# Moving operands that begin 12 bytes into their tiles, and another order of the three passes

## The chip, the core and the metric

The kernel runs on one core of one Trainium2 chip. The metric is the time of one execution on the device, in microseconds (us); a time is the median of several runs. Of the core's engines, TensorE multiplies (its rows read PE, and PEld for loading weights), VectorE (DVE), ScalarE (ACT) and GpSimd (POOL) work element by element, and SyncE (SP) and POOL issue most of the transfers (DMA) between the chip's memory and the on-chip memory, which has 128 partitions.

## What is computed

One step of a decoder layer in float32, for 512 tokens of a new sequence and 8 single tokens of running ones, 520 columns in all: a norm; a projection of 2048 channels to 6160 columns; a short gated convolution on one part and gated linear attention with 4 heads on the other; an output projection with residual; a norm; a gated feed-forward part with a causal convolution and 5632 channels; its down projection with residual; a last norm.

```python
def trunk(x, ...):
    m, c_new, s_new = mixer(rmsnorm(x, norm_mix_g[l]), ...)      # proj = xn @ w_in; out = concat(ya, yb) @ w_out
    x = x + m
    f, f_new = conv_ffn(rmsnorm(x, norm_ffn_g[l]), ...)          # u, v = split(xn @ w_up); h = silu(conv(u) + b) * v; h @ w_down
    x = x + f
    return rmsnorm(x, final_norm_g), ...
```

Nearly all the work is in four products: activations with `w_in`, `w_out`, `w_up` and `w_down`.

## The kernel before

**Three passes per product.** Every float32 number that goes into a large product is split in two parts of the type float32r: hi is the number rounded to it (ScalarE), lo what is left (VectorE). A product of weights w and activations x is then the sum of three matmuls, wh·xh + wh·xl + wl·xh, added up in one bank of the accumulator. In a matmul the weights, 128 x 128, are loaded into the array first (one LDWEIGHTS for each MATMUL in the program), and the activations move through it, 260 columns at a time: half of the 520. The activations are the *moving operand*. They lie in tiles of 128 partitions and T = 520 columns; the second half starts 260 columns, 1040 bytes, into the tile. As the program lays out its memory, each of these tiles starts at a multiple of 32 bytes in its partition, and so each half at a multiple of 16.

**Three places issue these passes.** `mm3` (L140) serves the first part of the kernel, the plain input projection, with two halves for each pass, and the last part, a remainder of the down projection in parts of 264 and 256 columns. `up_product` (L1218) serves the rest of the input projection ("mix") and the up projection, `chunk_product` (L1461) the output and the down projection. The latter two use a scheme with seven products instead of eight for a 2 x 2 block of matrices (Strassen's, in the form with few sums): a group of weights gives seven products, numbered in `ORDER`, each of 24 matmuls: eight steps of 128 rows, three passes each (`up_product`), or four steps with two column blocks (`chunk_product`).

**Which tiles move.** `pair_tiles` makes a pair of tiles, hi and lo, for the normed input (`bh`, `bl`, `ch`, `cl`, `xh`, `xl`). `form` gives the sums of activation blocks that the seven products need (`bh`, `yh`, `yl`, `b` in the profile's names); `load_form` loads such sums from memory, in the output and down projections, into tiles called `form`. The tiles of `form` and `load_form` share their places with others: those of `mixer_sums` ("yx") and the running sums `acc` of the projections. `tmp` is the pool of short-lived tiles. `keep_last` saves the last rows of the convolutions' inputs: it gathers them in a tile `last`, transposes it, copies it to `flat` on ScalarE and stores it.

**Order.** Behind the first part the order of each engine's work is written out: `prepare(i + 2)` makes the hi and lo parts of the weights two products ahead of their use, each product's `finish` empties the banks, and `run_steps` deals out the smaller work between products. A class `InOrder` fixes that order on TensorE, VectorE and ScalarE, later on POOL and SP too; in the first part a scheduler may still exchange steps.

Of the kernel before, what the change touches and what calls it, by code (L numbers as in the profile page):

```python
# [9 lines left out]
F32 = mybir.dt.float32  # L10
F32R = mybir.dt.float32r
# [6 lines left out]
P = 128  # L18
# [4 lines left out]
T = NP + NS  # L23
# [14 lines left out]
def trunk_kernel(  # L38
# [13 lines left out]
    tp = ctx.enter_context(tc.tile_pool(name="tmp", bufs=8))  # L52
# [37 lines left out]
                self.last[i.engine] = i.name  # L90

    def tmp():
        return tp.tile([P, T + 2], F32, tag="t", name="t")

    def two(ap):
        return ap.rearrange("p (a b) -> p a b", a=2)
# [34 lines left out]
    def halves(t):  # L131
        return t[:, :HT], t[:, HT:T]

    def mm3(outs, lhs, acts, first, last):

        wh, wl = lhs
        xh, xl = acts
        for i, (w, x) in enumerate(((wh, xh), (wh, xl), (wl, xh))):
            for o, xx in zip(outs, x):
                nc.tensor.matmul(o, w, xx, start=first and i == 0, stop=last and i == 2)  # L140

# [54 lines left out]
    bigA = actx.enter_context(tc.tile_pool(name="bigA", bufs=1, side="right"))  # L196
    bctx = ctx.enter_context(ExitStack())
    b12p = bctx.enter_context(tc.tile_pool(name="b12", bufs=1))

    def pair_tiles(pool, tag):  # L200

        return [pool.tile([P, T], F32R, tag=f"{tag[0]}{s}{tag[1:]}", name=tag[0] + s) for s in "hl"]

    xa, xw = [], {}
    for k in range(KD):
# [71 lines left out]
    with ExitStack() as es:  # L277
# [173 lines left out]
        for k in range(KD):  # L451
            c, t = k // 4, k % 4
# [117 lines left out]
    zp = actx.enter_context(tc.tile_pool(name="zpads", bufs=1, side="right"))  # L570
    yt1 = actx.enter_context(tc.tile_pool(name="yt1", bufs=1, side="right"))
# [4 lines left out]
    last = [None]  # L576
# [5 lines left out]
    def keep_last(z, j, n, new_p, new_s, get=None):  # L582

        jj = j % n
        if jj == 0:
            last[0] = zp.tile([P, 10, n], F32, tag=f"last{n}", name="last", bufs=2)
        if get:
            nc.scalar.activation(last[0][:, :, jj], z[:, NP:], AF.Copy)
        else:
            nc.gpsimd.tensor_copy(last[0][:, :, jj], z[:, NP:])  # L590
        if jj == n - 1:
            lt, c0 = last[0], (j - n + 1) * P

            def out():
                ps = (get or bank)()
                nc.tensor.transpose(
                    ps[: 10 * n, :P], lt.rearrange("p r j -> p (r j)"), idn
                )
                flat = zp.tile([110, P], F32, tag="flat", name="flat", bufs=2)
                nc.scalar.activation(flat[: 10 * n, :], ps[: 10 * n, :P], AF.Copy)  # L600
                for r in range(10):
                    dst = new_p[0, 0, r] if r < 2 else new_s[0, r - 2, 1]
                    (nc.gpsimd if get else nc.sync).dma_start(
                        dst[c0 : c0 + n * P].rearrange("(j p) -> j p", p=P),
                        flat[r * n : (r + 1) * n, :],
                    )

            soon.append(lambda: None)
            soon.append(out)
# [17 lines left out]
    slots = [None] * KD  # L627
    forms_d, xd = {"wo": g_d}, {}

    def load_form(kind, c, j):  # L630

        home = (7 * c + j) % 8
        if kind == "down" and home in (0, 7):
            home = 7 - home
        parts_ = []
        for x in range(2):
            tiles = []
            for q in range(2):
                t = slots[2 * home + q].tile(
                    [P, T], F32R, tag=f"y{'hl'[x]}{2 * home + q}", name="form"  # L640
                )
                pool = x == 1 if c == 0 else kind == "wo"
                (nc.gpsimd if pool else nc.sync).dma_start(
                    two(t.bitcast(F32)),
                    forms_d[kind][c][PLACE[ORDER[j]], x, 2 * q : 2 * q + 2].rearrange(
                        "i p c -> p i c"
                    ),
                )
                tiles += halves(t)
            parts_.append(tiles)  # L650
        xd[kind, c, ORDER[j]] = list(zip(*parts_))
# [11 lines left out]
    def acc_tag(n):  # L663
        return f"x{'hl'[n % 2]}{8 + n // 2}"
# [5 lines left out]
    def form(f, g):  # L670

        if f == 1:
            x = pair_tiles(bigA, f"b{g}")
        elif f in (2, 3):
            x = [
                bigA.tile([P, T], F32R, tag=acc_tag(4 * g + q), name="b2")
                for q in ((0, 3) if f == 2 else (1, 2))
            ]
        else:
            k = homes.get((f, g), {5: 0, 4: 4, 6: 8, 7: 12}[f] + g)  # L680
            x = [slots[k].tile([P, T], F32R, tag=f"y{s}{k}", name=f"y{s}{k}") for s in "hl"]
        for j, q in enumerate(zip(*(halves(y) for y in x))):
            xq[f, 2 * g + j] = q
        return x

    def first_tile(kind, g, m):

        return 4 * g + 2 * m if kind == "down" else 2 * g + 8 * m
# [6 lines left out]
    def mixer_sums():  # L695

        def place(n):
            return yt1.tile([P, T], F32, tag=f"y{n}", name="yx")  # L700

        for g in (1, 2, 3, 0):
            xg = [place(n) for n in ("l0 h8 l8 h0" if g % 2 else "l1 l4 h4 h0").split()]
            for q, x in enumerate(xg):
                nc.sync.dma_start(two(x), rows_of(xT_d, "mix", g, q))
            yield
            for q, x in enumerate(xg):
                m = first_tile("mix", g, q // 2)
                for j, h in enumerate(halves(x)):
                    nc.scalar.activation(h, h, AF.Copy, scale=gmix[:, m + j : m + j + 1])  # L710
                if q == 1:
                    yield
            yield
            t1, t3, t4, b22 = xg
            t2 = place("h1")
            sub(t1, t1, t3)
            minus(t2, t1, b22)
            yield
            if g:
                for f, t in ((5, t1), (4, t2)):  # L720
                    nc.gpsimd.dma_start(mt_d[f - 4, g], t)
            sub(t3, b22, t3)
            minus(t4, t2, t4)
            yield
            nc.gpsimd.dma_start(mt_d[3, g], t4)
            if g:
                nc.gpsimd.dma_start(mt_d[2, g], t3)
        for f, t in ((5, t1), (6, t3), (4, t2)):
            split(t, *form(f, 0))
# [32 lines left out]
    with ExitStack() as mix:  # L762
# [44 lines left out]
        with ExitStack() as gl:  # L807
# [263 lines left out]
            for h in range(NH):  # L1071
# [3 lines left out]
                k = gp.tile([P, T], F32, tag="qk", name="k", bufs=5)  # L1075
# [3 lines left out]
                q = gp.tile([P, T], F32, tag="qk", name="q", bufs=5)  # L1079
# [6 lines left out]
                for d in range(2):  # L1086
                    ps = group(w_in, 4096 + h * DV + d * P, xa, None if h + d else v0)
                    t = gp.tile([P, T], F32, tag="v", name="v", bufs=2)
# [119 lines left out]
    def up_product(i):  # L1208
        kind, at, r = order[i]
        st = state[kind, at]  # L1210
        b = BANK[r]
        if b not in st["bank"]:
            st["bank"][b] = mm_bank()[:, :HT]
        wh, wl = (x.rearrange("p (k c) -> p k c", k=8) for x in (his.pop(i), los.pop(i)))
        for k in range(8):
            xh, xl = xq[INPUT[r], k]
            for j, (w, x) in enumerate(((wh, xh), (wh, xl), (wl, xh))):
                nc.tensor.matmul(  # L1218
                    st["bank"][b], w[:, k, :], x, start=b not in st["used"] and k == 0 and j == 0,
                    stop=k == 7 and j == 2, skip_group_check=True,  # L1220
                )
        st["used"].add(b)
# [196 lines left out]

    def new_sums(g):  # L1420
        for q in range(4):
            acc[g, q] = bigA.tile([P, T], F32, tag=acc_tag(4 * g + q), name="acc")

    def load_residual(g):

# [21 lines left out]
    acc, dnp = {}, [None, None]  # L1447

    def chunk_product(i):
        kind, (c, g), r = order[i]  # L1450
        st = state[kind, (c, g)]
        b = BANK[r]
        if b not in st["bank"]:
            st["bank"][b] = two_banks("xy"[(g + (b == "c")) % 2])
        ps = inner(st["bank"][b])
        wh, wl = (x.rearrange("p (k c) -> p k c", k=4) for x in (his.pop(i), los.pop(i)))
        for k in range(4):
            xh, xl = xd[kind, c, r][k]
            for m in range(2):
                for j, (w, x) in enumerate(((wh, xh), (wh, xl), (wl, xh))):  # L1460
                    nc.tensor.matmul(  # L1461
                        ps[:, m, :], w[:, k, m * P : (m + 1) * P], x,
                        start=b not in st["used"] and k == 0 and j == 0,
                        stop=k == 3 and j == 2, skip_group_check=True,
                    )
        st["used"].add(b)
# [201 lines left out]
    for i, (kind, at, r) in enumerate(order):  # L1668
        j, n = i % 7, i // 7
# [41 lines left out]
        if i in (0, 2, NW, NW + 2):  # L1711

            x = xq[1, 0][0]
# [11 lines left out]
        if kind == "wo":  # L1725
            c, g = at
# [20 lines left out]
        if kind == "down":  # L1747
            c, g = at
# [157 lines left out]
```

## Time and profile before

| | us |
|---|---|
| median of 3 runs | 2180.16 |
| lowest, highest | 2179.63, 2182.27 |
| span of the profiled execution | 2180.4 |
| TensorE busy in it | 2152.9 (99%) |
| VectorE, ScalarE, POOL busy | 1735.7, 1114.0, 438.1 |

The profiled execution is the span between its first and its last instruction; nothing else is in its time. In the profile a line such as `L1218 PE MATMUL mm<-yl,hi 128*128 128x260 f32 x1696` says: at line 1218 TensorE multiplies the moving tile `yl` with the weights `hi` into the bank `mm`, 1696 times. Matmuls overlap each other in the pipeline: the 0.28 us that a row gives for one is longer than the distance between two starts, so it is the distance that counts, read from start times or from the number of matmuls in a window.

### The profile page before, as it was taken

The page shows a single profiled execution, that of the slowest core. Times are in us where ns is not written, and L with a number is a line of the kernel's source. Part 1 is how long each engine was busy: PE and PEld are TensorE (multiplying, and loading weights), DVE is VectorE, ACT ScalarE, POOL GpSimd, SP SyncE. Part 2 cuts the span into 40 slices and gives each one's busy share as a digit, 9 for nine tenths or more (in the row PEclk, how much of TensorE's full clock was granted, in tenths as well). Part 3 has the DMA queues.
Part 4 walks back from the last instruction along what each step waited for, and adds up shares of the span by engine and source line. Part 5 has one row for each costly group of instructions (what it writes and reads, how often), then busy time and mean ns, then how long its engine had stood idle before and what let it go on. Part 6 is the DMA issues. An engine that isn't in the chain of part 4 may idle for free.

```text
span 2180.4 us, 43803 instructions
## 1 busy us (share of the span) xinstructions
PE 2152.9 (99%) x17751; PEld 2131.3 (98%) x17751; DVE 1735.7 (80%) x2298; ACT 1114.0 (51%) x1625; POOL 438.1 (20%) x625
## 2 busy tenths in 40 slices
PE   9999999999999999999999999999999999999997
PEld 8999999999999999999999999999999999999997
DVE  6346465578888897988888988998998778888886
ACT  6335435355544586555555555555555553444445
POOL 4213131121243321121221131122111310010000
PEclk9999999999999999999999999999999999999999
DMA  8545464387788996667676676676677886894734
GB/s 247 147 125 158 122 191 124 92 246 210 204 257 248 297 266 176 179 178 187 164 189 174 165 195 176 163 194 177 171 186 190 285 202 197 248 271 132 226 107 156
DMA packets 467163, 415.51 MB, mean 191 GB/s; under 512 B 21641, under 2 KB 426393, under 8 KB 466817
## 3 DMA queue, kind: packets, MB, share of 16 engines
q1 hardware_dynamic: 424081, 289.71, 46.5%
q0 software_dynamic: 42832, 122.93, 21.4%
q8 instruction: 139, 2.28, 0.4%
q14 instruction: 63, 0.52, 0.1%
q10 hardware_dynamic: 48, 0.07, 0.0%
HBM read 299.45 MB, written 80.31 MB: 174 GB/s over the span
## 4 chain that ended last, share of the span: by engine, by line
PE 88%; DMA 4%; DVE 3%; issue 1%; ACT 1%; POOL 1%; SPq 0%; ACTq 0%; DVEq 0%; POOLq 0%
PE mm L1218 34%; PE mm L140 16%; PE ms L1218 14%; PE y L1461 7%; PE x L1461 7%; PE f L1461 3%; PE e L1461 3%; PE ms L957 1%; DMA raw<-in_w_out_dram 1%; DMA form<-g_d 1%; DVE lo L1198 1%; DMA g_d<-fh 1%; DMA x_d<-acc 1%; DMA yl<-t_d 0%; DMA raw<-in_w_down_dram 0%
## 5 line engine op out<-in xcount | busy, mean ns | idle before, releaser
L1218 PE MATMUL mm<-yl,hi 128*128 128x260 f32 x1696 | 479.8, 283 | 3.6 <-DVE yl L124 3.6
L1218 PE MATMUL mm<-yh,hi 128*128 128x260 f32 x1696 | 480.5, 283 | 2.1 <-ACT ms L1228 1.8
L1218 PE MATMUL mm<-yh,lo 128*128 128x260 f32 x1696 | 479.8, 283 | 0.8 <-DVE lo L1198 0.8
L1194 ACT ACTIVATE hi<-raw 128x1024 fp32r<-128x1024 f32 x324 | 342.6, 1057 | 233.9 <-PE mm L1218 69.0
L1198 DVE TENSOR_TENSOR lo<-raw,hi 128x1024 fp32r<-128x1024 f32 x324 | 395.2, 1220 | 41.2 <-ACT hi L1194 40.7
L1198 DVE TENSOR_TENSOR lo<-s,hi 128x1024 fp32r<-128x1024 f32 x243 | 298.3, 1228 | 127.2 <-ACT hi L1194 121.9
L1194 ACT ACTIVATE hi<-s 128x1024 fp32r<-128x1024 f32 x243 | 256.9, 1057 | 217.2 <-DVE s L1139 80.2
L1218 PEld LDWEIGHTS mm<-yl,hi 128*128 128x128 f32 x1696 | 320.1, 189 | 4.2 <-DVE yl L124 4.2
L1218 PEld LDWEIGHTS mm<-yh,hi 128*128 128x128 f32 x1696 | 319.7, 189 | 2.7 <-ACT ms L1228 2.0
L1218 PEld LDWEIGHTS mm<-yh,lo 128*128 128x128 f32 x1696 | 320.4, 189 | 1.2 <-DVE lo L1198 1.2
L1218 PE MATMUL ms<-b,hi 128*128 128x260 f32 x1408 | 257.8, 283 | 0.0
L1218 PEld LDWEIGHTS ms<-b,hi 128*128 128x128 f32 x1408 | 218.5, 190 | 0.0
L1461 PE MATMUL x<-form,hi 128*128 128x260 f32 x1120 | 204.6, 283 | 0.8 <-DVE acc L1480 0.8
L1461 PE MATMUL y<-form,hi 128*128 128x260 f32 x1120 | 204.5, 282 | 0.5 <-DVE acc L1480 0.5
L1139 DVE TENSOR_TENSOR s<-s,raw 128x1024 f32<-128x1024 f32 x162 | 197.8, 1221 | 2.8
L1218 PE MATMUL ms<-b,lo 128*128 128x260 f32 x704 | 199.5, 283 | 0.0
L1461 PEld LDWEIGHTS x<-form,hi 128*128 128x128 f32 x1120 | 172.4, 188 | 1.2 <-issue 1.0
L1461 PEld LDWEIGHTS y<-form,hi 128*128 128x128 f32 x1120 | 172.5, 188 | 0.8 <-issue 0.7
L1461 PE MATMUL y<-form,lo 128*128 128x260 f32 x560 | 158.2, 283 | 0.8 <-DVE lo L1198 0.8
L1461 PE MATMUL x<-form,lo 128*128 128x260 f32 x560 | 158.1, 282 | 0.0
L112 DVE TENSOR_TENSOR lo<-raw,hi 128x1024 fp32r<-128x1024 f32 x76 | 93.7, 1238 | 78.2 <-ACT hi L111 71.6
L1218 PEld LDWEIGHTS ms<-b,lo 128*128 128x128 f32 x704 | 133.4, 190 | 0.0
(366 smaller groups left out, 5077.8 us busy)
## 6 DMA issues: line engine op xcount, KB each, us to landing
raw<-in_w_up_dram SPq DMA_DIRECT2D x176, 512.0 KB, 4.7
raw<-in_w_down_dram SPq DMA_DIRECT2D x96, 512.0 KB, 5.5
raw<-in_w_in_dram SPq DMA_DIRECT2D x92, 512.0 KB, 4.4
form<-f_d SPq DMA_DIRECT2D x126, 260.0 KB, 6.8
raw<-raw POOLq DMA_DIRECT2D x56, 512.0 KB, 5.5
f_d<-t POOLq DMA_DIRECT2D x80, 260.0 KB, 5.5
raw<-in_w_out_dram SPq DMA_DIRECT2D x32, 512.0 KB, 12.7
form<-g_d POOLq DMA_DIRECT2D x42, 260.0 KB, 7.7
```

The source lines that it names most:

```text
L112: nc.vector.tensor_tensor(lo, raw, hi.bitcast(F32), op=ALU.subtract)
L140: nc.tensor.matmul(o, w, xx, start=first and i == 0, stop=last and i == 2)
L957: nc.tensor.matmul(pb[:, c * 64 : (c + 1) * 64], L[:, c, :], rhs[:, c], start=True, stop=True,)
L1139: return lambda: nc.vector.tensor_tensor(out, x, y, op=ALU.add)
L1194: nc.scalar.activation(his[i], src, AF.Copy)
L1198: nc.vector.tensor_tensor(los[i], src, his[i].bitcast(F32), op=ALU.subtract)
L1218: nc.tensor.matmul(st["bank"][b], w[:, k, :], x, start=b not in st["used"] and k == 0 and j == 0, stop=k == 7 and j == 2, skip_group_check ...
L1461: nc.tensor.matmul(ps[:, m, :], w[:, k, m * P : (m + 1) * P], x, start=b not in st["used"] and k == 0 and j == 0, stop=k == 3 and j == 2, ...
```

## The change

Two things. First, each tile that is a moving operand is made three columns wider, T + 3, and used from its fourth column: the operand begins 12 bytes into the tile. A helper, `moving`, does this for the pairs, the forms and the loaded forms; tiles that share a place with one of these are made wider too but used from their start. Three tiles are made smaller so that all fit: `tmp` loses two unused columns, `last` has one size for both convolutions, and `flat` has one buffer instead of two. Second, in all three places the passes run as wh·xh, wl·xh, wh·xl.

```diff
     def tmp():
-        return tp.tile([P, T + 2], F32, tag="t", name="t")
+        return tp.tile([P, T], F32, tag="t", name="t")
...
-        for i, (w, x) in enumerate(((wh, xh), (wh, xl), (wl, xh))):
+        for i, (w, x) in enumerate(((wh, xh), (wl, xh), (wh, xl))):
...
+    def moving(pool, tag, name):
+        return pool.tile([P, T + 3], F32R, tag=tag, name=name)[:, 3:]
...
-        return [pool.tile([P, T], F32R, tag=f"{tag[0]}{s}{tag[1:]}", name=tag[0] + s) for s in "hl"]
+        return [
+            moving(pool, f"{tag[0]}{s}{tag[1:]}", tag[0] + s) for s in "hl"
+        ]
...
-            last[0] = zp.tile([P, 10, n], F32, tag=f"last{n}", name="last", bufs=2)
+            last[0] = zp.tile([P, 110], F32, tag="last", name="last", bufs=2)[:, : 10 * n]
+            last[0] = last[0].rearrange("p (r j) -> p r j", j=n)
...
-                flat = zp.tile([110, P], F32, tag="flat", name="flat", bufs=2)
+                flat = zp.tile([110, P], F32, tag="flat", name="flat", bufs=1)
...
-                t = slots[2 * home + q].tile(
-                    [P, T], F32R, tag=f"y{'hl'[x]}{2 * home + q}", name="form"
-                )
+                t = moving(slots[2 * home + q], f"y{'hl'[x]}{2 * home + q}", "form")
...
-                bigA.tile([P, T], F32R, tag=acc_tag(4 * g + q), name="b2")
+                moving(bigA, acc_tag(4 * g + q), "b2")
...
-            x = [slots[k].tile([P, T], F32R, tag=f"y{s}{k}", name=f"y{s}{k}") for s in "hl"]
+            x = [moving(slots[k], f"y{s}{k}", f"y{s}{k}") for s in "hl"]
...
-            acc[g, q] = bigA.tile([P, T], F32, tag=acc_tag(4 * g + q), name="acc")
+            acc[g, q] = bigA.tile([P, T + 3], F32, tag=acc_tag(4 * g + q), name="acc")[:, :T]
```

The same exchange of passes stands in `up_product` and `chunk_product`. On TensorE, in the first product of `up_product` (the tiles `bh` and `bl` move, `hi` and `lo` are the weights), the program before has:

```order
L1218 MATMUL mm<-bh,hi 128x260
L1218 MATMUL mm<-bl,hi 128x260
L1218 MATMUL mm<-bh,lo 128x260
L1218 MATMUL mm<-bh,hi 128x260
L1218 MATMUL mm<-bl,hi 128x260
L1218 MATMUL mm<-bh,lo 128x260
```

and the changed one, whose lines stand five further down:

```order
L1223 MATMUL mm<-bh,hi 128x260
L1223 MATMUL mm<-bh,lo 128x260
L1223 MATMUL mm<-bl,hi 128x260
L1223 MATMUL mm<-bh,hi 128x260
L1223 MATMUL mm<-bh,lo 128x260
L1223 MATMUL mm<-bl,hi 128x260
```

The pass with `lo` has moved from the third place to the second, the pass with `bl` from the second to the third. In `mm3`, on TensorE near the start of the program, each pass runs over two tiles (`bh` and `ch`), so each moves by two places. Before:

```order
L140 MATMUL mm<-bh,hi 128x260
L140 MATMUL mm<-ch,hi 128x260
L140 MATMUL mm<-bl,hi 128x260
L140 MATMUL mm<-cl,hi 128x260
L140 MATMUL mm<-bh,lo 128x260
L140 MATMUL mm<-ch,lo 128x260
```

and now:

```order
L140 MATMUL mm<-bh,hi 128x260
L140 MATMUL mm<-ch,hi 128x260
L140 MATMUL mm<-bh,lo 128x260
L140 MATMUL mm<-ch,lo 128x260
L140 MATMUL mm<-bl,hi 128x260
L140 MATMUL mm<-cl,hi 128x260
```

The number of matmuls and of weight loads is the same.

More of the change, by code (lines that the diff above doesn't have):

```diff
@@ L699, in place @@
         def place(n):
-            return yt1.tile([P, T], F32, tag=f"y{n}", name="yx")
+            return yt1.tile([P, T + 3], F32, tag=f"y{n}", name="yx")[:, :T]
         for g in (1, 2, 3, 0):
@@ L1216, in up_product @@
             xh, xl = xq[INPUT[r], k]
-            for j, (w, x) in enumerate(((wh, xh), (wh, xl), (wl, xh))):
+            for j, (w, x) in enumerate(((wh, xh), (wl, xh), (wh, xl))):
                 nc.tensor.matmul(
@@ L1459, in chunk_product @@
             for m in range(2):
-                for j, (w, x) in enumerate(((wh, xh), (wh, xl), (wl, xh))):
+                for j, (w, x) in enumerate(((wh, xh), (wl, xh), (wh, xl))):
                     nc.tensor.matmul(
```

## The prediction

> **What bounds the kernel now.** I read the clock and the busy shares first, then the stretch of the span with the least other trouble in it, then the chain that ended last, then what TensorE waits for, and in the end single matmuls.
>
> ```profile
> core 0: 2180.4 us, clock 0.995
> ```
> ```profile
> PE 2152.9 (99%) x17751; PEld 2131.3 (98%) x17751; DVE 1735.7 (80%) x2298; ACT 1114.0 (51%) x1625; POOL 438.1 (20%) x625
> ```
> ```profile
> 1000.00:1400.00 400.00, 400.00 (x3342) 400.00 (x3342) 355.71 (x478) 217.69 (x322) 82.42 (x120) 1.00 0.68 178
> ```
>
> TensorE is busy for 99% of the span at a granted clock of 0.995, so the throttle is out of the question. In the window of the up projection (columns: window, length, then busy time and count of PE, PEld, DVE, ACT and POOL, then granted clock, DMA share, GB/s) it is busy for all of 400.00 us, with 3342 matmuls: one starts every 400.00 / 3342 = 119.7 ns. VectorE is next with 355.71 us, 89%.
>
> The chain that ended last says the same without the overlap of busy times: runs of 96 matmuls in 11.51 us, 119.9 ns each.
>
> ```profile
> 1000.22 11.51 PE mm L1218 x96
> 1020.35 11.51 PE mm L1218 x96
> ```
>
> How many matmuls are of the kind that the change touches? The three lines that run the products, over the whole span (columns: window, length, PE busy and count, PEld busy and count, clock, DMA share, GB/s), L1218, L1461 and L140 in this order:
>
> ```profile
> 0.00:2181.00 2181.00, 1074.78 (x8904) 1072.06 (x8904) 0.99 0.68 191
> ...
> 0.00:2181.00 2181.00, 566.05 (x4704) 564.53 (x4704) 0.99 0.68 191
> ...
> 0.00:2181.00 2181.00, 426.22 (x3264) 402.12 (x3264) 0.99 0.68 191
> ```
>
> That is 8904 + 4704 + 3264 = 16,872 matmuls. At 119.7 ns they make 2020 us of the 2180.4. So the change is priced in one unit: **1 ns on the spacing of these matmuls is 16.9 us, 0.77% of the time.** Waits can hardly matter. TensorE's longest, in total, are:
>
> ```profile
> PE mm L1218 <- DVE yl L124: 3.6, 3, 1.9
> PE mm L1218 <- ACT ms L1228: 1.8, 1, 1.8
> ...
> PE mm L140 <- DVE bl L127: 1.1, 2, 0.9
> ...
> PE mm L1218 <- DVE lo L1198: 0.8, 2, 0.5
> ...
> PE y L1461 <- DVE lo L1198: 0.8, 1, 0.8
> ...
> PE mm L140 <- DVE lo L112: 0.5, 1, 0.5
> ```
>
> **What sets the spacing.** If it were a fixed cost per instruction it would be the same for every operand. It is not. These are five starts in each of two products of the same kind (and the next start in the first), 377 us apart:
>
> ```profile
> 478.83 0.28 PE L1218 MATMUL mm<-yl,hi 128*128 128x260 f32 x1
> 478.95 0.30 PE L1218 MATMUL mm<-yh,lo 128*128 128x260 f32 x1
> 479.09 0.28 PE L1218 MATMUL mm<-yh,hi 128*128 128x260 f32 x1
> 479.21 0.28 PE L1218 MATMUL mm<-yl,hi 128*128 128x260 f32 x1
> 479.32 0.28 PE L1218 MATMUL mm<-yh,lo 128*128 128x260 f32 x1
> 479.44 0.28 PE L1218 MATMUL ms<-xh,hi 128*128 128x260 f32 x1
> ...
> 855.75 0.28 PE L1218 MATMUL mm<-yl,hi 128*128 128x260 f32 x1
> 855.87 0.30 PE L1218 MATMUL mm<-yh,lo 128*128 128x260 f32 x1
> 856.01 0.28 PE L1218 MATMUL mm<-yh,hi 128*128 128x260 f32 x1
> 856.13 0.28 PE L1218 MATMUL mm<-yl,hi 128*128 128x260 f32 x1
> 856.24 0.28 PE L1218 MATMUL mm<-yh,lo 128*128 128x260 f32 x1
> ```
>
> Starts follow each other by 0.12, 0.14, 0.12 and 0.11 us in the first product, and by the same four numbers in the second. The shape is the same in all of them; only the operands' places differ. So where the operands lie costs something: 0.14 us here, and from 479.21 to 479.44 two in a row take 0.23 us, 115 ns each. Each matmul reads 260 columns while the next weights (PEld) are read beside it. I take it that the two reads get into each other's way, and that the average of 119.7 ns holds some such delay. This is inferred: the page names no such wait.
>
> Width has a price too. Here are the first and the last of 12 consecutive matmuls of 264 columns, then of 12 of 256, in the last stage:
>
> ```profile
> 2112.75 0.28 PE L140 MATMUL mm<-bl,hi 128*128 128x264 f32 x1
> ...
> 2114.09 0.28 PE L140 MATMUL mm<-bh,hi 128*128 128x264 f32 x1
> ```
> ```profile
> 2142.33 0.28 PE L140 MATMUL mm<-bl,hi 128*128 128x256 f32 x1
> ...
> 2143.62 0.28 PE L140 MATMUL mm<-bh,hi 128*128 128x256 f32 x1
> ```
>
> 1.34 / 11 = 121.8 ns against 1.29 / 11 = 117.3 ns: 4.5 ns for eight columns. Counted in steps of four columns (16 bytes) it is 2.25 ns for one more step, or, in proportion (119.7 / 65), 1.84 ns.
>
> **The change, part by part.**
>
> *The 12 bytes.* Before, every moving operand starts at a multiple of 16 bytes in its partition (a half is 260 x 4 = 1040 bytes, so its second half does too); after, all start 12 bytes past one. No matmul, weight load or byte is added. No row of the profile has such an operand, so its cost is bounded from both sides. Upper end: the read now lies over 66 steps of 16 bytes in place of 65. If each step costs as above, that is +1.84 to +2.25 ns, 31 to 38 us slower. Lower end: the reads of columns and of the next weights no longer step together, and all matmuls go at the 115 ns of the undisturbed pair: -4.7 ns, 79 us faster (VectorE's 355.71 us would then be 93% of the shortened window, so it would not bind). The two ends lie on either side of zero. The row that I lean on is the repeated one, which shows that place alone moves a spacing by 20 to 30 ns out of 120; a shift that all operands have in common against the weights is a change of just that kind. I take the middle of the two ends, (-4.7 + 1.84) / 2 = -1.4 ns: 16,872 x -1.4 = **-24 us**.
>
> *The order of the passes.* A step of three ran wh·xh, wh·xl, wl·xh and now runs wh·xh, wl·xh, wh·xl. The count is the same, and each pass has its own weight load before and after (17751 of both). What moves is when a part is first needed: wl one pass earlier (two in L140, whose passes run over two halves), xl as much later. The four waits for lo in the rows above grow by 0.12 us each, the one of L140 by 0.24: +0.6 us. The five waits for yl and bl shrink by 3 x 0.12 + 2 x 0.24: -0.8 us. Elsewhere lo is made two products ahead (2 x 24 x 0.12 = 5.8 us), which covers it. Net **0**. As a tile xl is now the last one read, so its reload may start one pass, 0.12 us, later; hidden behind the same 5.8 us. If the order also changes how reads meet, that is inside the 12-byte term, since the bounds there are on the spacing as a whole.
>
> *The loads into shifted tiles.* The form tiles are loaded to places 12 bytes further on.
>
> ```profile
> form<-f_d SPq DMA_DIRECT2D x126, 260.0 KB, 6.8
> form<-g_d POOLq DMA_DIRECT2D x42, 260.0 KB, 7.7
> ...
>   DMA form<-g_d: 2.4, 5
> ```
>
> The last row is what TensorE's forms waited for: 2.4 us in 5 waits, all in the output projection. Their bytes stay the same: I take **0**. If an unaligned landing took twice as long, each of the five waits would grow by up to 7.7 us, 38 us; the 126 loads of the down projection are issued a whole chunk ahead and stay hidden.
>
> *The room made for it* (narrower tmp tiles, one tag for "last", one buffer for "flat"): the one new wait is ScalarE's copy to "flat" on the stores of the group before. In the up projection groups of 11 tiles are 11 x 20.13 us (the two chain rows) = 221 us apart, so the stores have long landed. **0.**
>
> Sum: 2180.4 - 24 + 0 + 0 + 0 = 2156 us. The profiled execution's 2180.4 and the median of 2180.16 agree within 0.3 us, so nothing is carried over.
>
> A rule speaks against this. The Trainium skill, in "SBUF — State Buffer", Specifications (TRN2), says that SBUF is read in lines of 16 bytes, that at least two hits on a line are needed for full bandwidth, and that each crossing to a new line costs. By it the shifted operand touches one line more, and the first line gives a single element; the time would be that of the first rival below. The width rows agree with a price per four columns; no run before this one has a shifted start.
>
> **Rivals.**
>
> *One more step per matmul (slower).* The place is every matmul of L1218, L1461 and L140. The read is the limit, each 16-byte step costs 1.84 ns, and 66 replace 65: 16,872 x 1.84 = +31 us, 2211 us. For it: 117.3, 119.7 and 121.8 ns for 256, 260 and 264 columns are near one ratio (0.458 to 0.461 ns a column), as if nothing but steps counted. Against it: a spacing of 110 to 140 ns at one width is no fixed price per step. It decides if the extra step is paid in full and the delays stay as they are.
>
> *Only reshuffled (no change).* The delays depend on many places at once; a common shift swaps long ones for short ones, and the mean over hundreds of places stays at 119.7: 2180 us, give or take 4. For it: in the chain the runs of 96 matmuls take the same 11.51 us, so the mean is steady. Against it: a common shift against the weights is not a random one.
>
> The Trainium skill has a rule for this case as well: "TensorE: Matmul & The Clock Gate", Step-by-step, says that weights have a read port of their own and take no bandwidth from the running matmul. By it the shift would change nothing. [...]
>
> *The loads become the wait (slower).* The 38 us above on an unchanged spacing: 2218 us, from the point where a form lands later than its product. Against it: loads of whole rows, and only five waits.
>
> **How the numbers follow.** Forecast 0.55, one more step 0.22, reshuffled 0.19, loads 0.04. The predicted time is the forecast's, 2156 us; its own range goes from 2101 (the lower end) to 2175. The range for all reaches up through no change to the slower cases, 2105 to 2205, and leaves out about 0.2. A difference of 0.2%, 4.4 us, is what a measurement of this kernel can tell. Faster: 0.55 and 0.03 of the reshuffled case, 0.58. Within 0.2%: 0.16, all but a little from reshuffling. Slower: 0.22, 0.02 and 0.02, 0.26.
>
> **What would show it.** In the window of the up projection the same 400 us should hold about 400 / 0.1183 = 3381 matmuls instead of 3342; the rival with one more step gives 400 / 0.1215 = 3292. Runs of 96 in the chain should take 11.38 us (rival: 11.69). Waits for lo and yl should differ by tenths of a microsecond, and waits for form should still be under 5 us. If the count per window stays at 3342 and the time moves all the same, the spacing was not the step and my reading is wrong.

## The result, and the profile after

The changed kernel takes 2171.28 us, the median of 5 runs (2168.1 to 2172.69), against 2181.0 us (5 runs, 2179.63 to 2182.27) for the kernel before on the same chip: a ratio of 0.9955, with the interval 0.9943 to 0.9966. It is faster by 9.7 us. The forecast was 24 us, two and a half times as much.

The span and clock of the changed kernel's profiled execution, and the busy times on its page:

```profile
core 0: 2169.2 us, clock 0.996
```
```profile
PE 2137.6 (99%) x17751; PEld 2114.4 (97%) x17751; DVE 1735.3 (80%) x2298; ACT 1112.6 (51%) x1625; POOL 440.2 (20%) x625
```

TensorE is still what the time hangs on, with the same 17,751 matmuls, and its busy time fell by 15.3 us (2152.9 to 2137.6), more than the span, which fell by 11.2 us. So part of what the matmuls gained was lost again between them. The same two stretches of the changed kernel, one in the up projection and one in the down projection (columns: window, length, busy time and count of PE, PEld, DVE, ACT and POOL, clock, DMA share, GB/s):

```profile
1000.00:1400.00 400.00, 400.00 (x3368) 400.00 (x3367) 358.83 (x482) 218.83 (x323) 83.34 (x120) 1.00 0.69 179
1900.00:2050.00 150.00, 150.00 (x1265) 150.00 (x1264) 127.64 (x128) 62.90 (x68) 8.01 (x11) 1.00 0.71 215
```

In the up projection 3368 matmuls fit where there were 3342: one per 118.8 ns instead of 119.7. In the down projection the kernel before has 1256 in its second window:

```profile
1900.00:2050.00 150.00, 150.00 (x1256) 150.00 (x1255) 125.40 (x128) 63.09 (x68) 9.20 (x12) 1.00 0.74 223
```

119.4 ns there became 118.6. The chain that ended last in the changed kernel (start, length, what) shows a run of 96 in 11.41 us, 118.9 ns each, where it was 11.51:

```profile
995.79 11.41 PE mm L1223 x96
```

For a finer measure I took, from the start times of all matmuls of 260 columns in the trace, the distance to the next one wherever it lies between 100 and 150 ns. The mean is 119.86 ns before and 118.94 after, 0.92 ns less; by the unit of the prediction that is 0.92 x 16.9 = 15.5 us. The spread shrank as well: the standard deviation of single distances went from 2.77 to 1.80 ns. The spot that the prediction quoted shows it. Single matmuls of the changed kernel's timeline, on the same moving tiles (start, length, what):

```profile
478.64 0.28 PE L1223 MATMUL mm<-yh,lo 128*128 128x260 f32 x1
478.75 0.28 PE L1223 MATMUL mm<-yl,hi 128*128 128x260 f32 x1
478.87 0.28 PE L1223 MATMUL mm<-yh,hi 128*128 128x260 f32 x1
478.99 0.28 PE L1223 MATMUL mm<-yh,lo 128*128 128x260 f32 x1
```

The starts follow by 0.11, 0.12 and 0.12 us. The 0.14 of before is gone, and there is no second 0.11 either.

What was given back is time in which TensorE stood idle, the span less its busy time: 2180.4 - 2152.9 = 27.5 us before and 2169.2 - 2137.6 = 31.6 us after, +4.1. Most of it stands in the waits of TensorE in the changed kernel (who waits for whom: total us, times, longest):

```profile
PE mm L1223 <- DVE yl L124: 4.1, 4, 1.7
PE y L1466 <- DVE lo L1203: 2.2, 1, 2.2
PE mm L1223 <- DVE lo L1203: 1.9, 3, 0.9
...
PE mm L140 <- DVE bl L127: 1.2, 2, 0.7
...
PE mm L140 <- DVE lo L112: 0.7, 1, 0.7
...
PE x L1466 <- DVE lo L1203: 0.3, 1, 0.3
```

The waits for lo add up to 2.2 + 1.9 + 0.7 + 0.3 = 5.1 us, against 0.8 + 0.8 + 0.5 = 2.1 before: +3.0. Those for yl and bl grew by 0.6 us (4.7 to 5.3). The longest, in the changed kernel's timeline, is at the border from the up to the down projection, where nothing has run two products ahead yet:

```profile
1800.53 0.39 PE L1466 MATMUL y<-form,lo 128*128 128x260 f32 x1 [2.22 <-DVE lo L1203]
```

The form tiles' loads on the changed kernel's page (KB each, median us from issue to landing):

```profile
form<-f_d SPq DMA_DIRECT2D x126, 260.0 KB, 6.2
...
form<-g_d POOLq DMA_DIRECT2D x42, 260.0 KB, 7.4
```

They land no later than before (6.8 and 7.7 us). Five waits stand beside these transfers, and they are not TensorE's: they are waits of POOL, which issues them, before and in the changed kernel:

```profile
POOL form L643 <- DMA form<-g_d: 2.4, 5, 0.9
...
POOL form L648 <- DMA form<-g_d: 3.7, 5, 2.3
```

Among the waits of TensorE in the two traces there is none for a transfer of a form tile.

One more thing stands in the two spans, and it is not the change: for stretches of a few microseconds TensorE was granted half of its clock, three times before and twice after. Windows around them, TensorE alone (window, length, busy and count, clock, DMA share, GB/s), before:

```profile
15.00:30.00 15.00, 14.13 (x92) 0.89 1.04 314
460.00:475.00 15.00, 12.38 (x87) 0.89 0.96 292
818.00:834.00 16.00, 12.65 (x76) 0.79 1.12 302
```

and in the changed kernel:

```profile
460.00:475.00 15.00, 12.00 (x84) 0.89 0.97 289
1795.00:1810.00 15.00, 12.78 (x94) 0.89 1.12 279
```

Inside such a stretch the clock is 0.50 (kernel before, 470 to 472 us), and the same matmuls start 0.21 to 0.22 us apart. By these shares 0.11 x 15 + 0.11 x 15 + 0.21 x 16 = 6.7 us of full clock are missing before and 3.3 us after, so up to 3.4 us of the difference of the spans can be due to the clock. The mean distance is free of this, since it leaves out distances over 150 ns, and so are the windows of 1000 and 1900 us, at a clock of 1.00.

So the two spans do not make an exact account. The spacing gives -15.5 us and the idle time +4.1, and the clock between 0 and -3.4; together that is -11.4 to -14.8, against -11.2 measured. What is left, 0.2 to 3.6 us, these rows do not place.

### The profile page after: what moved, and what is told of

Same layout as the page of the kernel before. It is cut to its first block, busy times and chain, and to the rows that moved or that the text cites. A ratio compares the mean times of both kernels' runs of the same rounds, so it can differ in the third digit from the quotient of the medians.

```text
span 2169.2 us, 43815 instructions
## 1 busy us (share of the span) xinstructions
PE 2137.6 (99%) x17751; PEld 2114.4 (97%) x17751; DVE 1735.3 (80%) x2298; ACT 1112.6 (51%) x1625; POOL 440.2 (20%) x625
## 4 chain that ended last, share of the span: by engine, by line
PE 60%; DMA 2%; DVE 1%; issue 1%; ACT 0%; POOL 0%; ACTq 0%; DVEq 0%; POOLq 0%; SPq 0%
PE mm L1223 28%; PE ms L1223 11%; PE y L1466 7%; PE x L1466 6%; PE e L1466 2%; PE f L1466 2%; PE mm L140 2%; DMA x_d<-acc 1%; DMA ssq<-fh 1%; DMA raw<-in_w_down_dram 0%; PE ms L1806 0%; DVE lo L1203 0%; DVE yl L124 0%; ACT y L1864 0%; DVE s L1144 0%
## 5 line engine op out<-in xcount | busy, mean ns | idle before, releaser
L1223 PE MATMUL ms<-b,hi 128*128 128x260 f32 x1408 | 265.7, 280 | 0.0
L1466 PE MATMUL y<-form,hi 128*128 128x260 f32 x1120 | 212.7, 282 | 1.3 <-DVE acc L1485 1.3
L1466 PE MATMUL x<-form,hi 128*128 128x260 f32 x1120 | 211.5, 281 | 0.1
L1466 PEld LDWEIGHTS y<-form,hi 128*128 128x128 f32 x1120 | 177.6, 189 | 1.8 <-ACT hi L1199 0.8
L1466 PEld LDWEIGHTS x<-form,hi 128*128 128x128 f32 x1120 | 176.6, 188 | 0.7 <-issue 0.5
L1466 PE MATMUL y<-form,lo 128*128 128x260 f32 x560 | 157.4, 281 | 2.2 <-DVE lo L1203 2.2
L1466 PE MATMUL x<-form,lo 128*128 128x260 f32 x560 | 156.7, 280 | 0.3 <-DVE lo L1203 0.3
```

Source lines behind the costliest of these rows:

```text
L1223: nc.tensor.matmul(st["bank"][b], w[:, k, :], x, start=b not in st["used"] and k == 0 and j == 0, stop=k == 7 and j == 2, skip_group_check ...
L1466: nc.tensor.matmul(ps[:, m, :], w[:, k, m * P : (m + 1) * P], x, start=b not in st["used"] and k == 0 and j == 0, stop=k == 3 and j == 2, ...
```

## The experiments

The theories behind the expectations: A, the shift counts because it moves the reads of the moving operand against those of the weights (the prediction's reading); B, the order of the passes alone does it; C, only both together; E, the rival's price of about 1.84 ns for each 16-byte step. D came up after the first runs: the operand's own start within 16 bytes counts, whatever the weights do.

**The change taken apart.** First the shift without the new order:

```diff
-for j, (w, x) in enumerate(((wh, xh), (wl, xh), (wh, xl))):
+for j, (w, x) in enumerate(((wh, xh), (wh, xl), (wl, xh))):
```

(in all three places), and then the new order without the shift, with every operand at the start of its tile, which is still three columns wider:

```diff
-return pool.tile([P, T + 3], F32R, tag=tag, name=name)[:, 3:]
+return pool.tile([P, T + 3], F32R, tag=tag, name=name)[:, 0 : 0 + T]
```

Expected of the shift alone:

> Moving operands 12 bytes in, passes in the old order (wh xh, wh xl, wl xh). The change as a whole took the spacing in the window of the up projection from 119.7 to 118.8 ns. Theory A (the shift alone does it, since columns and next weights no longer step together): about 118.8 ns, time about 2171 us. Theory B (the order alone does it): 119.7 ns, about 2181 us. Theory C (only together, since both move who reads what beside whom): between, or 2181 us.

and of the order alone:

> Moving operands at multiples of 16 bytes again (tiles still three columns wider), passes in the new order. Theory A (the shift): 119.7 ns, about 2181 us. Theory B (the order): 118.8 ns, about 2171 us. If the wider tiles alone do it by laying tiles out anew, this run also comes to about 2171 us.

The kernel before took 2179.29 us on the chip of these runs. The shift alone took 2172.82 us, a ratio of 0.997 (0.9959 to 0.9981). The order alone took 2184.69 us, 1.0021 (1.0012 to 1.003). The same two windows of the shift alone, from here on with the columns of the windows above:

```profile
1000.00:1400.00 400.00, 400.00 (x3352) 400.00 (x3352) 356.95 (x479) 217.23 (x321) 83.14 (x120) 1.00 0.68 179
1900.00:2050.00 150.00, 150.00 (x1263) 150.00 (x1263) 127.02 (x129) 63.10 (x68) 8.00 (x11) 1.00 0.71 216
```

and the first window of the order alone:

```profile
1000.00:1400.00 400.00, 400.00 (x3335) 400.00 (x3334) 355.37 (x477) 217.72 (x321) 82.28 (x120) 1.00 0.67 178
```

The mean distances are 119.30 ns (shift), 120.07 (order) and 118.94 (both), from 119.86. So B falls: alone, the order costs a little (with it the wider tiles, which lay the memory out anew, so these do not bring the gain either). The two do not add up: 0.997 x 1.0021 = 0.9991, while both together give 0.9955. With operands at 12 bytes the new order gains, and by the windows it does so in the up projection (3352 to 3368 matmuls) and hardly in the down projection (1263 to 1265). C has a share in the truth, A or D has the rest.

**The other starts.** The slice of the line above becomes `[:, 2 : 2 + T]` (8 bytes) and `[:, 1 : 1 + T]` (4 bytes), with the new order:

> As the changed kernel, but operands begin 8 bytes in. Theory A with any start inside a 16-byte step as good as another: 118.8 ns, about 2171 us. If what counts is how few columns the first step holds (one at 12 bytes, two at 8, three at 4): between 118.8 and 119.7 ns, about 2174 us. If one more step is paid in full somewhere: above 119.7 ns.

> As the changed kernel, but operands begin 4 bytes in. Any start inside a step as good as another: 118.8 ns, about 2171 us. If the first step's few columns count: about 119.4 ns, about 2178 us.

At 8 bytes the kernel took 2208.29 us, 1.0131 times the kernel before (1.0114 to 1.0148); at 4 bytes 2222.23 us, 1.0194 (1.0179 to 1.0209). The up projection's window of the kernel at 8 bytes:

```profile
1000.00:1400.00 400.00, 400.00 (x3288) 400.00 (x3287) 350.41 (x469) 213.25 (x312) 81.72 (x118) 1.00 0.66 176
```

and of the one at 4 bytes:

```profile
1000.00:1400.00 400.00, 400.00 (x3270) 400.00 (x3269) 348.90 (x468) 213.02 (x314) 78.67 (x115) 1.00 0.65 173
```

That is 121.7 and 122.3 ns in this window, 121.81 and 122.74 as means over the whole kernel. All three shifted starts touch 66 steps of 16 bytes. At 8 and 4 bytes the time is that of the rival "one more step" (2211 us) and beyond; at 12 bytes it is on the other side of no change. The step has its price, and 12 bytes escape it.

**Is it the place against the weights?** The weights' tiles are shifted by 12 bytes instead, with the moving operands at 0, and then both:

```diff
-his[i] = wp.tile([P, 1024], F32R, tag="hi", name="hi")
+his[i] = wp.tile([P, 1024 + 3], F32R, tag="hi", name="hi")[:, 3:]
```

(and the same for the lo tiles and for the weights of `mm3`).

> As the changed kernel, but moving operands at multiples of 16 bytes and the weights' hi and lo parts 12 bytes in. Starts of 0, 4, 8 and 12 bytes gave spacings of 120.1, 122.7, 121.8 and 118.9 ns. Theory A (what counts is the moving operand's start against the weights' start): the operand is 4 bytes past the weights, modulo 16, so about 122.7 ns, 2222 us. Theory D (what counts is the moving operand's own start, in steps of 16 bytes): 120.1 ns, about 2184 us, and what the weights' shift costs by itself.

> Moving operands and weights both 12 bytes in. Theory A (start against start): as with both at 0, about 120.1 ns, 2184 us. Theory D (the operand's own start): 118.9 ns, about 2171 us.

One run each, beside 2180.86 us for the kernel before: 2185.51 us with the weights alone shifted, 2169.64 us with both. The window with the weights alone:

```profile
1000.00:1400.00 400.00, 400.00 (x3333) 400.00 (x3332) 355.19 (x478) 217.61 (x321) 82.52 (x120) 1.00 0.67 178
```

and with both:

```profile
1000.00:1400.00 400.00, 400.00 (x3367) 400.00 (x3366) 358.76 (x481) 218.86 (x323) 83.15 (x120) 1.00 0.68 179
```

3333 matmuls is the kernel with the order alone (3335); 3367 is the changed kernel (3368). If the place against the weights counted, the second should have lost the gain. It did not: A falls, D stands.

**The same without the layer.** The following kernels run only groups of matmuls in place of the layer, 480 in a row into one output tile (960 and 288 in two of them), on 16 moving and 16 weight slices in turn. The spacing is (busy time of the group less one matmul's 0.28 us) / (count - 1). Each of these kernels ran once. The first varies the starts of either operand:

```diff
+bench("new_m_zero", 0, 0, "new")
+bench("new_m_twelve", 3, 0, "new")
+bench("new_w_twelve", 0, 3, "new")
+bench("new_both_twelve", 3, 3, "new")
...
```

The numbers are the start of the moving operand and that of the weights, in elements of 4 bytes; the word is the order of the passes.

> Not the layer: 14 groups of 480 matmuls of 260 columns each, from two tiles of weights and one of moving columns, nothing else running; the outputs are not the reference's. Groups old_m_* and new_m_*: moving start 0, 4, 8, 12 bytes with either order; new_w_*: weights start 4, 8, 12; new_both_*: both. If the reads of columns and weights alone make the spacing, the order of the four starts is that of the kernel: 4 slowest, then 8, 0, and 12 fastest, over some 4 ns. Theory A: new_both_* all equal the start of 0, and new_w_twelve, w_eight, w_four equal m_four, m_eight, m_twelve. Theory D: new_both_* equal new_m_*, and new_w_* the start of 0. If the groups do not differ at all, the rest of the kernel (other engines, transfers) is part of the cause.

Its windows restricted to one group each (columns: window, length, busy time and count of PE, PEld and DVE, clock, DMA share, GB/s): the new order with both at 0, moving operand at 4, 8 and 12, weights at 12, both at 12:

```profile
0.00:834.00 834.00, 57.79 (x480) 57.69 (x480) 0.43 (x1) 1.00 0.02 6
...
0.00:834.00 834.00, 58.88 (x480) 58.78 (x480) 0.43 (x1) 1.00 0.02 6
...
0.00:834.00 834.00, 58.70 (x480) 58.61 (x480) 0.43 (x1) 1.00 0.02 6
...
0.00:834.00 834.00, 57.42 (x480) 57.33 (x480) 0.43 (x1) 1.00 0.02 6
...
0.00:834.00 834.00, 57.78 (x480) 57.69 (x480) 0.43 (x1) 1.00 0.02 6
...
0.00:834.00 834.00, 56.99 (x480) 56.90 (x480) 0.43 (x1) 1.00 0.02 6
```

Spacings of 120.1, 122.3, 122.0, 119.3, 120.0 and 118.4 ns. The first four repeat the whole kernels (120.07, 122.74, 121.81, 118.94) to within half a nanosecond; the weights' start alone does nothing. D again, outside of the layer, with one spot that it does not cover: with both at 12 bytes the spacing lies 0.9 ns under that of the moving operand alone at 12. The whole kernels do not show this (means of 118.97 and 118.94 ns).

**What the weights have to do with it.** The second group kernel reads fewer weight columns, other widths, and one operand all the time (behind the order stand the columns of the moving operand and of the weights):

```diff
+bench("cfull_m_zero", 0, 0, "new", 260, 128)
+bench("cquarter_m_zero", 0, 0, "new", 260, 32)
+bench("ne_m_zero", 0, 0, "new", 512)
+bench("same_m_zero", 0, 0, "new", 260, 128, same=True)
...
```

> Not the layer: 18 groups of 288 matmuls, outputs not the reference's. For starts of 0 and 12 bytes: 128, 64 and 32 weight columns (cfull, chalf, cquarter), widths of 256, 264, 384 and 512 columns (nb to ne), and one and the same operand and weights all the time (same). If the delay over the width's own time comes from the weights' reads, fewer weight columns shorten the spacing, and the gain of the start of 12 bytes shrinks with them; the delay is then the same number of ns at 512 columns as at 256. If it is a price per 16-byte step, it grows with the width and does not care for the weights.

Its windows for 128 and 32 weight columns, moving operand at 0:

```profile
0.00:736.00 736.00, 34.75 (x288) 34.65 (x288) 0.43 (x1) 1.00 0.02 7
...
0.00:736.00 736.00, 34.17 (x288) 31.05 (x288) 0.42 (x1) 1.00 0.02 7
```

120.1 and 118.1 ns: with a quarter of the weight columns the matmuls run 2 ns closer. At 12 bytes it is 119.3 and 117.7. With a single operand read over and over the four starts (0, 4, 8, 12) give 119.3, 122.3, 121.5 and 117.8 ns, so the effect is not one of changing tiles. Between 256 and 512 columns (118.0 and 232.1 ns at start 0) a column costs 0.45 ns. What 12 bytes gain on start 0 grows with the width, 0.6 ns at 256 columns, 1.8 at 384 and 2.1 at 512 (from the starts of the matmuls), so it is not a sum saved once per matmul.

**Start and width together.** If steps of 16 bytes are the price, widths of 256 to 264 columns at the four starts must fall on one line. The third kernel runs 5 widths x 4 starts with 128 weight columns, the fourth the same with 32 (the order is now spelled out: hh is wh times xh, lh is wl times xh, hl is wh times xl):

```diff
+bench("nc_twelve", 3, 0, "hh lh hl", 260)
...
+bench("nc_twelve", 3, 0, "hh lh hl", 260, 32)
```

> Not the layer: 20 groups of 480 matmuls, nothing else running; outputs not the reference's. Starts of 0, 4, 8 and 12 bytes (names end so), widths of 256, 258, 260, 262 and 264 columns (na, nb, nc, nd, ne). If each 16-byte step touched has a price (theory E), the spacing follows the number of steps: at a start of 0, 64 steps for 256, 65 for 258 and 260, 66 for 262 and 264; at 4 bytes 65, 65, 66, 66, 67; at 8 bytes 65, 65, 66, 66, 67; at 12 bytes 65, 66, 66, 67, 67; so jumps where the number goes up and 12 never better than 4. If it is where the first step begins (theory D: one column alone in the first step is cheap, two or three are dear), all widths shift by the same: 12 bytes under 0, 4 and 8 bytes above, by the kernel's -0.9, +2.9 and +1.9 ns at every width. If it is where the last step ends, the best start changes with the width.

> As micro_c with 32 weight columns instead of 128. If the four starts differ through the weights' reads, they come within 0.5 ns of each other here; if through the moving operand's reads alone, they differ as in micro_c (12 under 0 by about 1 ns, 4 and 8 above by 2 to 3 ns).

From the 128-column kernel, windows of single groups: 260 columns at 0 and 12 bytes:

```profile
0.00:1180.00 1180.00, 57.82 (x480) 57.72 (x480) 0.43 (x1) 1.00 0.02 5
...
0.00:1180.00 1180.00, 57.10 (x480) 57.01 (x480) 0.43 (x1) 1.00 0.02 5
```

All twenty spacings in ns, with the number of 16-byte steps touched in brackets:

| start | 256 | 258 | 260 | 262 | 264 |
|---|---|---|---|---|---|
| 0 | 117.8 (64) | 119.8 (65) | 120.1 (65) | 121.7 (66) | 121.2 (66) |
| 4 bytes | 120.6 (65) | 120.5 (65) | 122.8 (66) | 122.0 (66) | 124.3 (67) |
| 8 bytes | 120.2 (65) | 119.7 (65) | 121.9 (66) | 121.9 (66) | 123.5 (67) |
| 12 bytes | 117.3 (65) | 118.5 (66) | 118.6 (66) | 119.6 (67) | 121.0 (67) |

In the first three rows the number of steps decides, to within some 1.6 ns: means of 120.2 ns for 65, 121.9 for 66, 123.9 for 67, 1.85 ns a step. Those in the last row lie 2.9 to 4.3 ns below the mean of the same number of steps. So 12 bytes are not a shift like the others: they pay less than their steps, by more than the extra step costs.

The kernel with 32 weight columns, windows of its groups of 260 columns at 0 and at 12 bytes:

```profile
0.00:1180.00 1180.00, 56.85 (x480) 51.75 (x480) 0.42 (x1) 1.00 0.01 3
...
0.00:1180.00 1180.00, 56.70 (x480) 51.55 (x480) 0.42 (x1) 1.00 0.01 3
```

The expectation had two outcomes, and neither came. The two groups have 118.1 and 117.8 ns, 0.3 apart, where 128 weight columns have 1.5 (at 4 and 8 bytes it is 121.1 and 120.0). Over the five widths the means differ from start 0 by +2.6, +0.9 and -0.1 ns (4, 8, 12 bytes), where 128 weight columns give +1.9, +1.3 and -1.1. The loss at 4 bytes is there with few weights too; the gain of 12 bytes on start 0 is nearly gone. But what sets 12 bytes apart is not: against the other starts with the same number of steps they are still 1.9 to 3.5 ns under the mean (128 weight columns: 2.9 to 4.3), though the other starts spread more here, from 117.0 to 120.1 ns for 65 steps. So about 1 ns of the advantage goes with the weights, and the larger part does not. Whether that 1 ns is a matter of the weights' reads is not shown, since fewer weight columns also give fewer rows of the result.

**The order by itself.** Six orders of the three passes, each at 0 and at 12 bytes, 960 matmuls a group:

```diff
+bench("oa_zero", 0, 0, "hh hl lh")
+bench("ob_zero", 0, 0, "hh lh hl")
+bench("oc_zero", 0, 0, "lh hh hl")
...
```

> Not the layer: 12 groups of 960 matmuls of 260 columns, outputs not the reference's. Starts of 0 and 12 bytes, the six orders of the passes (oa: wh xh, wh xl, wl xh as before; ob: wh xh, wl xh, wh xl as changed; oc: wl xh, wh xh, wh xl; od: wh xl, wh xh, wl xh; oe: wl xh, wh xl, wh xh; of: wh xl, wl xh, wh xh). If the order matters by repeating an operand or weights, oa differs from ob by about +0.4 ns at 12 bytes and -0.2 ns at 0, as in the kernel, and orders that repeat both (oc, od) stand out. If order only deals the places out anew, all six agree within 0.2 ns and the kernel's difference belongs to its places.

Windows of single groups: the order before and the new one at 0, then the two at 12 bytes:

```profile
0.00:1400.00 1400.00, 115.30 (x960) 115.20 (x960) 0.43 (x1) 1.00 0.01 4
...
0.00:1400.00 1400.00, 115.49 (x960) 115.40 (x960) 0.43 (x1) 1.00 0.01 4
...
0.00:1400.00 1400.00, 114.23 (x960) 114.13 (x960) 0.43 (x1) 1.00 0.01 4
...
0.00:1400.00 1400.00, 114.03 (x960) 113.94 (x960) 0.43 (x1) 1.00 0.01 4
```

119.93 and 120.14 ns at 0, 118.82 and 118.61 at 12 bytes: the new order costs 0.21 ns at 0 and gains 0.21 at 12. In the whole kernels it is +0.21 and -0.36, the same signs. All six orders lie within 119.53 to 120.14 at 0 and 118.47 to 118.89 at 12.

The first group kernel held the same two orders on moving slices that lie elsewhere (2112 bytes apart instead of 2240), and there the signs are the other way round. Its groups in the order before, at 0 and at 12 bytes:

```profile
0.00:834.00 834.00, 57.92 (x480) 57.82 (x480) 0.43 (x1) 1.00 0.02 6
...
0.00:834.00 834.00, 57.16 (x480) 57.07 (x480) 0.43 (x1) 1.00 0.02 6
```

They make 120.3 and 118.7 ns, against 120.1 and 119.3 with the new order: the new order gains 0.28 at 0 and costs 0.55 at 12. So the start within 16 bytes does not settle what an order does; it changes with the places of the tiles, and that the last group kernel has the signs of the whole kernel may be chance.

**A version with the best of both?** Since the new order gained only in the up projection, and the longest new wait is in a product of the down projection, this kernel has the new order in the up projection alone, with the 12 bytes everywhere:

```diff
-for j, (w, x) in enumerate(((wh, xh), (wl, xh), (wh, xl))):
+for j, (w, x) in enumerate(((wh, xh), (wl, xh), (wh, xl)) if kind == "up" else ((wh, xh), (wh, xl), (wl, xh))):
```

> Moving operands 12 bytes in, the new order in the up projection alone, the old one everywhere else. In the up projection the new order took 0.56 ns off the spacing at 12 bytes (59.42 against 59.70 us for 500 matmuls), in the down projection nothing; at the borders of the stages TensorE's waits for lo grew by 3 us with it. If the waits are due to the order: they return to the 2 us of before and the time is 2 to 3 us under the changed kernel, about 2169 us. If they come from the faster TensorE itself: about 2171 us.

It took 2169.34 us against 2178.54 on its chip: 0.9955 (0.9942 to 0.9969), the changed kernel's ratio. Its window has the same 3368 matmuls. Its longest wait of TensorE for lo:

```profile
PE y L1466 <- DVE lo L1203: 2.0, 1, 2.0
```

and that of the kernel with the shift and the old order throughout:

```profile
PE y L1466 <- DVE lo L1203: 0.9, 2, 0.8
```

The long wait at L1466 stays at 2.0 us though the product that waits has its old order back, and it is 0.8 us where the up projection has the old order. In the kernel with the new order throughout and no shift the same wait is short as well:

```profile
PE mm L1223 <- DVE lo L1203: 1.6, 3, 0.8
...
PE mm L140 <- DVE lo L112: 0.8, 1, 0.8
PE y L1466 <- DVE lo L1203: 0.6, 1, 0.6
```

So it does not come from needing lo one pass earlier. It goes with the fastest up projection ahead of it. The timelines of the kernel with the old order throughout and of this one show the wait itself (idle time before it in brackets):

```profile
1802.91 0.39 PE L1466 MATMUL y<-form,lo 128*128 128x260 f32 x1 [0.76 <-DVE lo L1203]
```
```profile
1800.19 0.39 PE L1466 MATMUL y<-form,lo 128*128 128x260 f32 x1 [2.02 <-DVE lo L1203]
```

TensorE is ready for lo at 1802.15 us in the first and at 1798.17 in the second, 4.0 us earlier; lo comes only 2.7 us earlier. My reading is that TensorE gains more on the way to the border than VectorE, 90% busy in the window of the up projection (358.83 of 400 us in the changed kernel), can follow; that reading is argued from these rows, and no run changed VectorE's part.

## Why the prediction was right or wrong

**The direction and the unit held.** The spacing of the 16,872 matmuls is what moved, by the count per window (3368, between the 3381 of the forecast and the 3342 of before, far from the rival's 3292) and by the runs of 96 (11.41 us; forecast 11.38). The time, 2171 us, lies in the forecast's own range of 2101 to 2175, near its upper end. But that the sign came out right was luck: the same working holds for starts of 4 and 8 bytes, which touch 66 steps as well, and there the kernel is 1.9% and 1.3% slower.

**The step that failed is the term "the 12 bytes".** It was put at -1.4 ns, the middle between a full extra step (+1.84) and the pair of 115 ns. Alone the shift measured -0.56 ns, with the order -0.92: -24 us became -15.5 us of spacing. The middle of two distant bounds was no measurement, and the lower bound was too hopeful: the 115 ns pair was a short distance next to a long one, and in the changed kernel both have moved to about 0.12 us. The reading under it, that a common shift moves the reads against the weights, fell outright: shifting the weights alone changed nothing, and shifting both kept the gain. What counts is where the moving operand starts within 16 bytes. The half of the reading that said "the two reads get into each other's way" has a little support: a quarter of the weight columns brings the spacing down by 2 ns at start 0 and takes about 1 ns off the advantage of 12 bytes, while 1.9 to 3.5 ns of it remain. Why 12 bytes escape, where 4 and 8 do not, stays open; it is measured in whole kernels and in groups, and explained in neither.

**"One more step per matmul" had the right price and the wrong case.** 1.84 ns was read from proportion, 1.85 was measured at the starts of 0, 4 and 8 bytes. Two of the three possible shifts behave as it says (2208 and 2222 us for its 2211). Had the change used 8 bytes, this rival would have been the result. The rule of the Trainium skill behind it ("SBUF — State Buffer", Specifications) agrees with the trace in that each crossing to a new 16-byte line costs. It does not agree in what follows for a line with one hit: by it 260 columns from 12 bytes, with one column on the first line, should cost no less than from 8 bytes, with two on the first and two on the last, and the runs have 118.6 against 121.9 ns.

**The order of passes was not 0.** The prediction left its effect on the reads "inside the 12-byte term"; in these kernels it is +0.21 ns alone and -0.36 ns on top of the shift, so that four tenths of the spacing gain hang on it, and the group kernels show that it goes with the places of the tiles. Its effect on waits was also wrong: +0.6 us for lo and -0.8 us for yl and bl were forecast; measured are +3.0 and +0.6 (4.7 to 5.3). Sized as "one pass earlier", the lo term would have been about right for the order alone, whose lo waits are 1.6 + 0.8 + 0.6 = 3.0 us, +0.9. The rest comes only where TensorE is faster too: most likely it runs into the same VectorE at the borders, where the cover of two products ahead does not exist. That a faster TensorE waits more can be seen from the other side too. The span less TensorE's busy time is 23.3 us in the kernel with 4 bytes, 24.3 with 8, 27.5 before and 31.6 after: what is slower on TensorE waits less, what is faster waits more.

**Loads and room at 0 held.** The loads into shifted places land in 6.2 and 7.4 us (6.8 and 7.7 before), and TensorE waits for none of them; the rival of late loads did not happen. The prediction read its row of five waits, 2.4 us, wrongly, though: they are POOL's, not TensorE's (3.7 us after), so the rival's price of 38 us had no such wait to grow from. ScalarE's copies to "flat" waited for matmuls (5.3 us in 4 waits, 0.4 in a fifth) and for no store.

**"Only reshuffled"** fails, since each of the four starts has a spacing of its own that comes back in other kernels. The rule that the prediction set beside it (the Trainium skill, "TensorE: Matmul & The Clock Gate", Step-by-step: the weights' reads take nothing from the running matmul) does not cover the runs, 120.1 ns with 128 weight columns against 118.1 with 32; whether it is the reads that make the difference is not shown.

Of the 14.7 us between the forecast and the measured gain (24.4 and 9.7), 8.9 are the spacing (24.4 less 15.5) and 4.1 TensorE's idle time. The last 1.7 are not placed; the clock of the profiled executions stands in them, since the medians gained 9.7 us and the profiled pair 11.2.

## What to carry to other kernels

Where TensorE is full with float32r matmuls of some 260 columns, the start of the moving operand within 16 bytes is a setting like any other: in this kernel its four values span 2.4% of the time, and a group of 480 matmuls without the rest of the kernel tells them apart beforehand, which no reasoning from rows at a single start did. The order of passes is worth tenths of a nanosecond and must be tried in the kernel itself, together with the start, as the effects do not add and the groups do not agree on it. Price a gain on the spacing by count times nanoseconds, then take off what TensorE waits more, here 4.1 of 15.5 us. Before closing an account between two profiled executions, look at the granted clock of each: here it could hide 3.4 us. And where a view lists waits beside a tile, look whose they are.

## What was not expected of the hardware

- One row of the table is out of line with the three others: a moving operand that begins 12 bytes past a multiple of 16 costs 2.9 to 4.3 ns less than its 16-byte steps, at every width from 256 to 264 (1.9 to 3.5 with 32 weight columns).
- The loss is largest at 4 bytes (122.8 ns), less at 8 (121.9), though both touch the same number of steps as 12.
- The weights' own start by itself plays no part (120.0 ns at 12 bytes, 120.1 at 0), while their number of columns does (2 ns from 128 to 32).
- The order of three passes with the same operands moves the spacing by tenths of a nanosecond, at 0 as at 12 bytes up in one layout of the slices and down in another.
